# One head's gate projections move from the recurrence to the block stage, by way of DRAM

## The chip, the cores and the metric

The kernel runs on one core of a Trainium2 chip, in float32. The metric is the device time of one execution in microseconds. Five engines work from queues of their own: TensorE (PE; its weight loads are PEld), VectorE (DVE), ScalarE (ACT), GpSimd (POOL) and SyncE (SP), which here only starts transfers. An instruction waits for the semaphores of those it depends on, and the ones behind it on its engine wait with it.

## The reference

One layer of a hybrid encoder block on 1024 tokens of width 1024. One normalised input `h` goes through one wide input projection, whose columns are cut into an attention branch (three groups of eight heads) and a bidirectional gated recurrence of eight heads. The change concerns the recurrence's forget gates, `zf_fwd` and `zf_bwd`:

```
h = rms_norm(h_res, norm_w[layer])
z = einsum('bsd,dc->bsc', h, w_in[layer])
qkv_a, g_a, q_b, zf_fwd, zf_bwd, i_b, g_b, zgate_a, zgate_b = split(z, split_points)
...
def hgrn2_scan(q, i, z_f, lb):
    f = lb + (1.0 - lb) * sigmoid(z_f)
    return gla_chunk_scan(q, 1.0 - f, i, log(f))
o_fwd = hgrn2_scan(q_b, i_b, zf_fwd, lb_f)
o_bwd = flip(hgrn2_scan(flip(q_b), flip(i_b), flip(zf_bwd), lb_b))
o_b = rms_norm(o_fwd + o_bwd, hg_norm_w[layer]) * silu(g_b)
...
merged = sigmoid(zgate_a) * y_a + sigmoid(zgate_b) * y_b
```

`gla_chunk_scan` works on chunks: cumulative sums of the logarithms, products of queries and keys with their exponentials, a state passed from chunk to chunk.

## The kernel before

A float32 product is made from three matmuls of split operands: each operand is a high part (fp32r) and the low rest, and high x high, low x high and high x low are summed. So the 8 blocks of 128 of the inner dimension cost 24 matmuls for each 128 x 512 result.

The stages follow each other on TensorE. First the value projections; then the **block stage** (`run_quads`), in which a "quad", a 2 x 2 block product (two token halves by two column blocks), is made with 7 products of 12 matmuls instead of 8, from sums of the input halves and differences of weight blocks that DVE makes. The block stage makes attention queries and keys, sigmoid gates, SiLU gates and the query projections of six heads of the recurrence, and stores them in DRAM; its list is `blocks`, its weights come in tiles `qraw`, and its results stand in PSUM as `qA`, `qE` and `qC` and leave it as `stage` or `spare`. After it come attention, the merge of its groups, the **recurrence**, and the end stage (projections of both branches, `y_a` first, then the gates and the output product).

In the recurrence TensorE makes, head by head, the four gate projections of a head (two directions `d` by two token halves `u`, `T_group`: 24 matmuls `gp` each). ACT copies each out of PSUM to a tile `sk` of a ring of seven (`evac_f`, `sk_ring`), and after the fourth `start_head` starts the head's chain: ACT makes the sigmoids and, after a change of its function table, the logarithms (`logs`); DVE the running sums (`sums`, tile `Bc`); ACT the exponentials (`exps_b`); DVE the products (`k_mul`, `q_mul`) and, once the decay is known (`decay`), the scaled keys, written over `sk` (`k_state`); TensorE transposes these (`kT`), which frees the `sk` slot, and makes the states (`U`), the products within chunks (`X`, `Y`), the outputs (`oB`) and, after ACT and DVE have normalised them (`on`, `ssb`, `oy`, `oz`), the output transpositions (`onT`). These small products stand between the projections of later heads. Behind the projections of head 7 follow eight groups of the second sigmoid gate (`evac_sg`), and then `y_a`, whose operands (`acc`, split to `xh` and `xl`) are loaded by `end_start`, which runs when all heads are out.

The order on every engine is made while the program is built. A planner (`Plan`) keeps a clock for each engine; tasks and small products (`task`, `product`) are put in when their operands should be there and their ring has room (`soon`); a projection whose result finds no free slot holds the builder at `until`, which lets small products and tasks go ahead. On the chip the order is fixed, and only real dependences make an engine wait.

Heads are counted from 0, so the seventh is head 6. Key transpositions are made strictly in order of the heads (`k_next`). The ring of seven is filled in the order of the `get` calls, so that a tile's slot is that of the tile seven before it. Nearly all instructions are recorded through one helper, line 58, so that the rows of the profile are told apart by the names of their tiles.

Of the kernel before, what the change touches and what calls it, by code (L numbers as in the profile page):

```python
# [8 lines left out]
F32 = mybir.dt.float32  # L9
# [18 lines left out]
TAIL, LATE = 4, 4  # L28
EARLY = 8
QB = 6  # L30
QRAW, SPARE = 6, 7
LOWS = ("T2", "T4")
SQ, EA = 2, 6
# [3 lines left out]
def _dram(ap, offset, dims):  # L37
    return bass.AP(tensor=ap.tensor, offset=ap.offset + offset, ap=dims)
# [584 lines left out]
def hybrid_block(ctx, tc, a, out):  # L623
    b = Builder(ctx, tc, a)
    a_, v_, g_, t_, s_ = b.p.act, b.p.dve, b.p.pool, b.p.pe, b.p.sp
# [4 lines left out]
    dr = ctx.enter_context(tc.tile_pool(name="scratch", bufs=1, space=DRAM))  # L630
# [32 lines left out]
    zf_pages = lambda h: some(head_page(h), 4)  # L663
    ib_pages = lambda k: [_dram(wi, (100 + 40 * k + d) * 65536, [[512, 128], [20 * 65536, 2], [1, 256]]) for d in range(8)]
    q_pages = lambda h: some(head_page(h) + (4 if h % 2 else 12), 2)
    gate_pages = lambda w, j: some((80, 176)[w] + 2 * j, 2)
    qk = [("qk", g, hv, e) for g in range(3) for hv in range(2) for e in range(2)]
    sg = [("sg", 0, j) for j in range(0, 8, 2)] + [("sg", 1, j) for j in range(0, TAIL, 2)]
    blocks = []
    for k in range(6):  # L670
        blocks += qk[2 * k:2 * k + 2] + sg[k:k + 1] + ([("qb", 2 * k - 2)] if 0 < k <= QB // 2 else [])
    blocks += [("gb", k) for k in range(4)] + [("ga", 0), ("ga", 2)]

    def block_pages(kind, *at):
        if kind == "sg":
            return (*gate_pages(*at), *gate_pages(at[0], at[1] + 1))
        if kind == "ga":
            return tuple(some(72 + 2 * at[0], 4))
        if kind == "qb":
            return (*q_pages(at[0]), *q_pages(at[0] + 1))  # L680
        if kind == "gb":
            return tuple(_dram(wi, (100 + 20 * at[0] + 4 * k) * 65536 + 256 + 128 * col, [[512, 128], [65536, 4], [1, 128]])
                         for col in range(2) for k in range(2))
        g, hv, e = at
        p = 24 * g + 8 + 8 * hv
        return tuple(_dram(wi, (p + 4 * k) * 65536 + 128 * (2 * e + col), [[512, 128], [65536, 4], [1, 128]])
                     for col in range(2) for k in range(2))

    items = some(0, 8) + some(24, 8) + some(48, 8)
    items += [block_pages(*x) for x in blocks]  # L690
    for k in range(2):
        items += ib_pages(k)
    for h in range(QB, EARLY):
        items += q_pages(h)
    for j in range(TAIL, LATE):
        items += gate_pages(1, j)
    for h in range(8):
        items += zf_pages(h) + (q_pages(h) if h >= EARLY else [])
    for j in range(LATE, 8):
        items += gate_pages(1, j)  # L700
    items += [wpa[i] for i in range(8)]
# [149 lines left out]
    obD = dr.tile([8, 2, 128, 512], F32, name="obD")  # L851
    ibD = dr.tile([2, 8, 128, 512], F32, name="ibD")
    qD = dr.tile([EARLY, 2, 128, 512], F32, name="qD")
    gbD = dr.tile([8, 2, 128, 512], F32, name="gbD")
    vD = dr.tile([3, S, 512], F32, name="vD")
    qkD = dr.tile([3, 2, 4, 128, S], F32, name="qkD")
# [38 lines left out]
    def T_group(p0, half, evac, last):  # L895
        def step(d):
            wh, wl = b.w[p0 + d // 4]
            c = 128 * (d % 4)
            xh, xl = hs(0, d, 512 * half, 512), hs(1, d, 512 * half, 512)
            return [(wh[:, c:c + 128], xh), (wh[:, c:c + 128], xl), (wl[:, c:c + 128], xh)]  # L900

        gr = dict(k=8, step=step, evac=evac, need=lambda d: p0 + d // 4 + 1)
        if last:
            gr["free"] = lambda d: p0 + (d + 1) // 4
        return gr
# [71 lines left out]
    def root(k):  # L977
        rs[k] = inv_rms(k, bank("ss"))
        rs["d", k] = spread(rs[k])

    def root_out(k):
        rs["B", k] = spread_out(rs["d", k])
# [18 lines left out]
    at = {0: {11: lambda: root(1)}, 3: {5: lambda: root_out(1), 11: lambda: root(0)}, 7: {5: lambda: root_out(0)}}  # L1001
# [174 lines left out]
    def put_raw(dst, silu=False):  # L1176
        def f(half, col, z, mine):
            ring = stage
            if not mine:
                ring, ps, z = blk["spare"], z, blk["spare"].get()  # L1180
                a_.activation(z, ps, AF.Silu if silu else AF.Copy)

            def out():
                s_.dma_start(dst(col, half), z)
                ring.done(z)

            if mine and silu:
                b.task("act", [z], lambda: (a_.activation(z, z, AF.Silu), b.task("sp", [z], out, 1)), 2)
            else:
                b.task("sp", [z], out, 1)  # L1190
        return f

    put_sg = lambda w, j: put_raw(lambda col, half: sgD[w, j + col, half])
    put_ga = lambda j: put_raw(lambda col, half: gaD[j + col, half], True)
    put_qb = lambda h: put_raw(lambda col, half: qD[h + col, half])
    put_gb = lambda k: put_raw(lambda col, half: gbD[2 * k + col, half], True)

    A = {op: [[hq[e][tk][:, c] for c in range(4)] for e in range(2)]
         for op, tk in {"11": (0, 0), "21": (0, 1), "T4": (1, 1)}.items()}
    for op, k in {"T1": 0, "T2": 1, "T3": 2, "22": 3}.items():  # L1200
        A[op] = [[x[:, c] for c in range(4)] for x in blk["S"][k]]
    b.BACK = 1.2
    b.run_quads(A, [{"qk": put_qk, "sg": put_sg, "ga": put_ga, "gb": put_gb, "qb": put_qb}[x[0]](*x[1:]) for x in blocks],
                [blk["spare"] if x[0] == "qk" else stage for x in blocks])
    b.BACK = 2.5
    pos += 7 * len(blocks)
# [377 lines left out]
    for pr in range(2):  # L1584
# [8 lines left out]
        pos += 8  # L1593
    for h in range(QB, EARLY):
        for u in range(2):
# [32 lines left out]
    sk_ring = b.ring(hp, "sk", 7, [128, 512])  # L1628
# [5 lines left out]
    SK, QQ = {}, {}  # L1634

    def evac_f(h, d, u):
        def f(ps):
            t = sk_ring.get()
            a_.activation(t, ps, AF.Copy)
            b.gps.done(ps)  # L1640
            SK[h, d, u] = t
            if d == 1 and u == 1 and h:
                start_head(h)
        return f
# [31 lines left out]
    def load_q_early(h, u):  # L1676
        t = qq_ring.get()
        s_.dma_start(t, qD[h, u])
        QQ[h, u] = t

    def load_gb(h, u):
        t = gb_ring.get()
        s_.dma_start(t, gbD[h, u])
        GB[h, u] = t

    def evac_q(h, u):
        def f(ps):
            t = qq_ring.get()
            a_.activation(t, ps, AF.Copy)
            b.gps.done(ps)  # L1690
            QQ[h, u] = t
        return f

    ORDER = ((0, 0), (0, 1), (1, 1), (1, 0))
# [5 lines left out]
    def start_head(h):  # L1700
        st = dict(used={}, mm=[None, None], G=[None, None], QR={}, Q2={}, KM={}, S={}, s=0, qm=0, km=0)
        H[h] = st
        for d in range(2):
            st["mm"][d] = mm_ring.get()
        b.task("act", [SK[h, d, u] for d, u in ORDER], lambda: logs(h), 4, lambda: qr_ring.soon(4))

    def logs(h):
        for d, u in ORDER:
            a_.activation(SK[h, d, u], SK[h, d, u], AF.Sigmoid)
        ln_exp()  # L1710
        for d, u in ORDER:
            lf = qr_ring.get()
            a_.activation(lf, SK[h, d, u], AF.Ln, scale=omlb[:, d, h:h + 1], bias=lb[:, d, h:h + 1])
            b.task("dve", [lf], lambda d=d, u=u, lf=lf: sums(h, d, u, lf), 4, q2_ring.soon)
# [247 lines left out]
    def load_pair(pr):  # L1962
        for i in range(8):
            b.task("sp", [ibD], lambda i=i: load_ig(pr, i), 4, ig_ring.soon)

    b.low = "dma"
    for h in range(8):
        if h % 2 == 0:
            load_pair(h // 2)
        for u in range(2):  # L1970
            if h < EARLY:
                b.task("sp", [qD], lambda h=h, u=u: load_q_early(h, u), 4, qq_ring.soon)
            b.task("sp", [gbD], lambda h=h, u=u: load_gb(h, u), 4, gb_ring.soon)
        if h == 0:
            start_head(0)
            continue
        for d in range(2):
            for u in range(2):
                b.run_unit([T_group(pos, u, evac_f(h, d, u), u == 1)])
            pos += 2  # L1980
        if h >= EARLY:
            for u in range(2):
                b.run_unit([T_group(pos, u, evac_q(h, u), u == 1)])
            pos += 2
# [423 lines left out]
def _build(arrays):  # L2408
    import concourse.bacc as _bacc
    nc = _bacc.Bacc("TRN2", target_bir_lowering=False, num_devices=1)  # L2410
    args = {n: nc.dram_tensor(f"in_{n}_dram", v.shape, mybir.dt.from_np(v.dtype), kind="ExternalInput").ap()
            for n, v in arrays.items()}
    out = nc.dram_tensor("out_0_dram", (S, D), F32, kind="ExternalOutput").ap()
    with tile.TileContext(nc) as tc:
        hybrid_block(tc, args, out)
    return nc
# [9 lines left out]
```

## Time and profile before

| | |
|---|---|
| median of 2 runs | 1455.42 us (1455.40 to 1455.44) |
| the profiled execution, its own time | 1454.89 us |
| its span, first to last instruction | 1453.1 us |
| instructions | 22946 |
| matmuls | 7930 |
| DMA issues from SP for weight pages of the block stage (`qraw`) | 108 of 256 KB |
| for weight pages of the direct projections (`raw` from `w_in`) | 84 of 256 KB |

In a row of a timeline stand the start in us from the span's start, the length in us, engine, line, operation, output tile <- input tiles, shapes, a count where equal instructions are merged, and in brackets the idle time before it with what ended it. Busy time counts overlapping instructions of one engine once; matmuls overlap, so that the time from the start of one to the start of the next is shorter than the length of one.

### The profile page before, as it was taken

The page shows a single profiled execution, that of the slowest core. Times are in us where ns is not written, and L with a number is a line of the kernel's source. Part 1 is how long each engine was busy: PE and PEld are TensorE (multiplying, and loading weights), DVE is VectorE, ACT ScalarE, POOL GpSimd, SP SyncE. Part 2 cuts the span into 40 slices and gives each one's busy share as a digit, 9 for nine tenths or more (in the row PEclk, how much of TensorE's full clock was granted, in tenths as well). Part 3 has the DMA queues.
Part 4 walks back from the last instruction along what each step waited for, and adds up shares of the span by engine and source line. Part 5 has one row for each costly group of instructions (what it writes and reads, how often), then busy time and mean ns, then how long its engine had stood idle before and what let it go on. Part 6 is the DMA issues. An engine that isn't in the chain of part 4 may idle for free.

```text
span 1453.1 us, 22946 instructions
## 1 busy us (share of the span) xinstructions
PE 1444.3 (99%) x7930; PEld 1197.2 (82%) x7930; DVE 968.1 (67%) x1901; ACT 894.9 (62%) x1900; POOL 340.3 (23%) x356
## 2 busy tenths in 40 slices
PE   9999999999999999999999999999999999999998
PEld 8788888888888888888888778888888888788887
DVE  6673678678685788331564649487878786358973
ACT  7743767466565676443688852497777784558461
POOL 0102434464523433333002000031222221001011
PEclk9999999999999999999999999999999999999999
DMA  7746567777643334324848449354444453778665
GB/s 238 181 143 196 165 195 162 192 153 170 148 123 102 98 105 114 111 102 144 280 144 282 151 118 326 123 141 105 126 109 125 110 138 75 225 240 220 181 154 136
DMA packets 194992, 230.75 MB, mean 159 GB/s; under 512 B 46083, under 2 KB 118043, under 8 KB 194364
## 3 DMA queue, kind: packets, MB, share of 16 engines
q1 hardware_dynamic: 180188, 203.93, 45.0%
q0 software_dynamic: 13824, 25.17, 11.7%
q8 instruction: 62, 1.02, 0.3%
q14 instruction: 54, 0.44, 0.1%
q10 hardware_dynamic: 864, 0.19, 0.1%
HBM read 169.29 MB, written 81.43 MB: 173 GB/s over the span
## 4 chain that ended last, share of the span: by engine, by line
PE 90%; DVE 5%; ACT 3%; DMA 1%; issue 1%; SPq 0%; POOL 0%; ACTq 0%; DVEq 0%
PE gp L58 25%; PE qA L58 20%; PE qE L58 10%; PE sA L58 6%; PE qC L58 5%; PE sE L58 5%; PE u L58 3%; PE o L58 3%; PE oB L58 3%; PE pT L58 2%; PE sc L58 2%; PE nss L58 2%; DVE Bc L58 1%; PE U L58 1%; DVE S L58 1%
## 5 line engine op out<-in xcount | busy, mean ns | idle before, releaser
L58 POOL TENSOR_TENSOR wlo<-qraw,whi 128x512 fp32r<-128x512 f32 x135 | 194.3, 1444 | 381.8 <-ACT whi L58 293.8
L58 ACT ACTIVATE whi<-qraw 128x512 fp32r<-128x512 f32 x189 | 117.7, 626 | 100.8 <-DVE qraw L58 43.1
L58 DVE TENSOR_TENSOR qraw<-qraw,qraw 128x512 f32<-128x512 f32 x108 | 100.0, 927 | 39.0 <-POOL wlo L58 28.0
L58 PE MATMUL gp<-hh,whi 128*128 128x512 f32 x264 | 109.7, 416 | 0.0
L58 PE MATMUL gp<-hh,wlo 128*128 128x512 f32 x264 | 103.6, 393 | 0.0
L58 PE MATMUL gp<-hl,whi 128*128 128x512 f32 x264 | 103.0, 390 | 0.0
L58 ACT ACTIVATE as<-as,neg 128x192 f32<-128x192 f32 (+2 forms) x192 | 83.8, 442 | 16.8 <-DVE neg L58 16.7
L58 ACT ACTIVATE whi<-raw 128x512 fp32r<-128x512 f32 x92 | 57.6, 627 | 43.8 <-PE gp L58 18.7
L58 PE MATMUL qA<-hh,whi 128*128 128x512 f32 x216 | 84.4, 391 | 0.0
L58 PE MATMUL qA<-hh,wlo 128*128 128x512 f32 x216 | 84.3, 390 | 0.0
L58 DVE CUSTOM_DVE_ANT_0 as<-sc,abias 128x192 f32<-128x192 f32 (+2 forms) x192 | 56.0, 348 | 42.4 <-PE sc L58 27.1
L58 PE MATMUL qA<-hl,whi 128*128 128x512 f32 x216 | 84.0, 389 | 0.0
L58 POOL COPY mm<-Bc 128x8 f32<-128x8 f32 x64 | 32.2, 534 | 205.6 <-DVE Bc L58 123.6
L58 PE MATMUL gp<-whi,hh 128*128 128x512 f32 x192 | 78.6, 409 | 0.0
L58 PE MATMUL gp<-wlo,hh 128*128 128x512 f32 x192 | 75.2, 391 | 0.4 <-DVE wlo L58 0.4
L58 PE MATMUL gp<-whi,hl 128*128 128x512 f32 x192 | 75.0, 391 | 0.0
L58 DVE TENSOR_TENSOR wlo<-qraw,whi 128x512 fp32r<-128x512 f32 x54 | 37.3, 691 | 49.6 <-ACT whi L58 49.6
L58 DVE SCALAR_TENSOR_TENSOR ny<-ny,spare 128x512 f32<-128x512 f32 x48 | 67.4, 1405 | 1.6
L58 ACT ACTIVATE ny<-ny 128x512 f32<-128x512 f32 x96 | 60.8, 633 | 4.0 <-DVE ny L58 0.8
L58 PEld LDWEIGHTS gp<-hh,wlo 128*128 128x128 f32 x264 | 49.5, 188 | 11.0
L58 POOL DMA_DIRECT2D wlo<-in_w_in_dram x36 | 31.5, 875 | 113.6 <-ACT wlo L58 97.8
L58 PEld LDWEIGHTS gp<-hh,whi 128*128 128x128 f32 x264 | 49.8, 188 | 8.3
(306 smaller groups left out, 4208.2 us busy)
## 6 DMA issues: line engine op xcount, KB each, us to landing
qraw<-in_w_in_dram SPq DMA_DIRECT2D x108, 256.0 KB, 3.8
raw<-in_w_in_dram SPq DMA_DIRECT2D x84, 256.0 KB, 3.7
qkD<-ny SPq DMA_DIRECT2D x48, 256.0 KB, 2.8
wlo<-in_w_in_dram POOLq DMA_DIRECT2D x36, 256.0 KB, 4.4
sg<-sgD SPq DMA_DIRECT2D x32, 256.0 KB, 3.7
eraw<-wsD SPq DMA_DIRECT2D x32, 256.0 KB, 3.3
sgD<-stage SPq DMA_DIRECT2D x26, 256.0 KB, 2.7
ak<-qkD SPq DMA_DIRECT2D x6, 1024.0 KB, 6.6
```

Source lines behind the costliest of these rows:

```text
L58: got = f(*args, **kw)
```

## The change

The four gate projections of head 6 are made as one quad of the block stage (its two column blocks are the two directions), stored in a DRAM tensor `zfD`, and loaded to `sk` tiles in the recurrence. The loads are tasks of SP with the condition that the ring has room; the head starts when its four tiles are there. The loop of the recurrence goes straight on to head 7. Head 6's four pages of weights leave the list of the direct projections, so the pages behind them move up by four.

```
+ZB = (6,)
...
     for k in range(6):
         blocks += qk[2 * k:2 * k + 2] + sg[k:k + 1] + ([("qb", 2 * k - 2)] if 0 < k <= QB // 2 else [])
+    blocks += [("zf", h) for h in ZB]
     blocks += [("gb", k) for k in range(4)] + [("ga", 0), ("ga", 2)]
...
+        if kind == "zf":
+            return tuple(zf_pages(at[0]))
...
-        items += zf_pages(h) + (q_pages(h) if h >= EARLY else [])
+        items += (zf_pages(h) if h not in ZB else []) + (q_pages(h) if h >= EARLY else [])
...
+    zfD = dr.tile([8, 2, 2, 128, 512], F32, name="zfD")
...
+    put_zf = lambda h: put_raw(lambda col, half: zfD[h, col, half])
...
+    def load_f(h, d, u):
+        t = sk_ring.get()
+        s_.dma_start(t, zfD[h, d, u])
+        SK[h, d, u] = t
+        if all((h, *k) in SK for k in ORDER):
+            start_head(h)
...
         if h == 0:
             start_head(0)
+            continue
+        if h in ZB:
+            for d, u in ORDER:
+                b.task("sp", [zfD], lambda h=h, d=d, u=u: load_f(h, d, u), 4, sk_ring.soon)
             continue
```

The same planner makes a new order of it. On SP, where the kernel before has these rows in the recurrence (stores of outputs `obD`, pages `raw`, gates `gb`, queries `q`, values `ig`):

```order
L58 DMA obD_163<-stage_96_11458 128x512
L58 DMA raw_83_11489<-in_w_in_dram 128x512
L58 DMA gb_11_11491<-gbD_166 128x512
L58 DMA q_12_11538<-qD_165 128x512
L58 DMA q_13_11540<-qD_165 128x512
L58 DMA obD_163<-stage_97_11574 128x512
L58 DMA raw_84_11585<-in_w_proj_a_dram 128x512
L58 DMA gb_12_11587<-gbD_166 128x512
L58 DMA raw_85_11647<-in_w_proj_a_dram 128x512
L58 DMA raw_86_11741<-in_w_proj_a_dram 128x512
```

the changed kernel has these, with the third and fourth of head 6's loads (tiles 28 and 30 of the ring `sk`):

```order
L59 DMA obD_163<-stage_99_11570 128x512
L59 DMA gb_11_11597<-gbD_167 128x512
L59 DMA sk_28_11599<-zfD_166 128x512
L59 DMA q_12_11659<-qD_165 128x512
L59 DMA q_13_11661<-qD_165 128x512
L59 DMA obD_163<-stage_100_11685 128x512
L59 DMA gb_12_11738<-gbD_167 128x512
L59 DMA sk_30_11740<-zfD_166 128x512
L59 DMA raw_83_11803<-in_w_proj_a_dram 128x512
```

Each load stands behind the store of an output and a load of a gate; the page loads have moved, by their four places and behind the loads.

On ACT, the chain of head 6 begins before the change with these rows: the copy of its last projection (tile 27) out of PSUM, a page's split, a table load, and the sigmoids of tiles 24 to 27.

```order
L58 ACTIVATE sk_27_11530<-gp618_11460 128x512
L58 ACTIVATE whi_269_11534<-raw_80_11096 128x512
L58 ACTIVATE wlo_269_11535<-whi_269_11534 128x512
L58 ACT_TABLE_LOAD
L58 ACTIVATE sk_24_11185<-sk_24_11185 128x512
L58 ACTIVATE sk_25_11301<-sk_25_11301 128x512
L58 ACTIVATE sk_27_11530<-sk_27_11530 128x512
L58 ACTIVATE sk_26_11441<-sk_26_11441 128x512
L58 ACT_TABLE_LOAD
```

With the change the sigmoids are those of the loaded tiles 24, 26, 28 and 30, and the copy ahead of them (tile 29) is already that of head 7's third projection.

```order
L59 ACTIVATE sk_29_11735<-gp622_11603 128x512
L59 ACT_TABLE_LOAD
L59 ACTIVATE sk_24_11284<-sk_24_11284 128x512
L59 ACTIVATE sk_26_11381<-sk_26_11381 128x512
L59 ACTIVATE sk_28_11599<-sk_28_11599 128x512
L59 ACTIVATE sk_30_11740<-sk_30_11740 128x512
L59 ACT_TABLE_LOAD
```

Behind them stand the four logarithms (`qr`), of which the next rows show the last, and then, on ACT still, the squares of head 5's two outputs (`on`), the splits of two weight pages (`whi`, `wlo`) and the small steps of the norm (`oy`, `oz`):

```order
L59 ACTIVATE qr_27_11769<-sk_30_11740,lbv_9145,omlb_9146 128x512
L59 ACTIVATE on_10_11789<-oB635_11777 128x512
L59 ACTIVATE whi_275_11797<-raw_79_11194 128x512
L59 ACTIVATE wlo_275_11798<-whi_275_11797 128x512
L59 ACTIVATE on_11_11832<-oB638_11820 128x512
L59 ACTIVATE whi_276_11841<-raw_80_11239 128x512
L59 ACTIVATE wlo_276_11842<-whi_276_11841 128x512
L59 ACTIVATE oy639_11846<-ssb636_11801,eps_82 128x4
```

Then come the small steps of the second output, two sets of four exponentials of head 6 (`km`, `qr`, `q2`), the scalings of head 5's two outputs (`on`) and the exponential of head 6's first decay (`G`). So head 6 now shares its stretch of ACT with head 7's copies, and its sigmoids wait for a transfer, with head 5's outputs behind them.

At the end of the recurrence SP has, before, the last two stores of outputs, a store of the second gate (`sgD`), the loads of the attention's result (`acc`, eight, of which two are shown):

```order
L58 DMA obD_163<-stage_108_12605 128x512
L58 DMA obD_163<-stage_109_12633 128x512
L58 DMA sgD_162<-stage_110_12641 128x512
L58 DMA acc_0_12657<-oaD_161 128x512
L58 DMA acc_1_12659<-oaD_161 128x512
```

and with the change:

```order
L59 DMA sgD_162<-stage_111_12637 128x512
L59 DMA obD_163<-stage_112_12649 128x512
L59 DMA obD_163<-stage_113_12675 128x512
L59 DMA sgD_162<-stage_114_12690 128x512
L59 DMA acc_0_12698<-oaD_161 128x512
L59 DMA acc_1_12700<-oaD_161 128x512
```

Before, one more store of the gate followed behind the eight loads; the last store of the gate stands ahead of them now; on TensorE 30 matmuls of the gate stood behind the last `onT` before the change, and 12 stand there with it.

More of the change, by code (lines that the diff above doesn't have):

```diff
@@ L1202, in hybrid_block @@
     b.BACK = 1.2
-    b.run_quads(A, [{"qk": put_qk, "sg": put_sg, "ga": put_ga, "gb": put_gb, "qb": put_qb}[x[0]](*x[1:]) for x in blocks],
+    b.run_quads(A, [{"qk": put_qk, "sg": put_sg, "ga": put_ga, "gb": put_gb, "qb": put_qb, "zf": put_zf}[x[0]](*x[1:]) for x in blocks],
                 [blk["spare"] if x[0] == "qk" else stage for x in blocks])
```

## The prediction

> **What bounds the kernel now.** I read the page first, then TensorE's matmul rate in the chain of waits, the busy time by stretches of the recurrence, the timelines of TensorE and ScalarE there, and last the hand-over to the end stage.
>
> ```profile
> span 1453.1 us, 22946 instructions
> PE 1444.3 (99%) x7930; PEld 1197.2 (82%) x7930; DVE 968.1 (67%) x1901; ACT 894.9 (62%) x1900; POOL 340.3 (23%) x356
> PE   9999999999999999999999999999999999999998
> ```
>
> TensorE is busy in every slice, so at first sight every matmul saved is time saved. In the chain of waits (start, duration, piece) is the price of one: 24 back to back take 5.44 us in the block stage and 30 take 6.83 us in the recurrence, 0.227 and 0.228 us each (the 390 ns of a group's row is the length of one, and they overlap).
>
> ```profile
> 153.70 5.44 PE qA L58 x24
> 1000.50 6.83 PE gp L58 x30
> ```
>
> The next rows are stretches: length, busy us of PE, PEld, DVE, ACT, POOL with instruction counts, granted clock, DMA. The first is the block stage; the other five run from head 4's first key transposition (kT) to the last output transposition (onT), cut at the kT marks shown below them.
>
> ```profile
> 150.00:680.00 530.00, 530.00 (x2330) 437.05 (x2329) 355.96 (x427) 323.02 (x551) 217.16 (x168) 1.00 0.52 137
> 1103.80:1135.60 31.80, 31.66 (x233) 27.39 (x232) 27.04 (x60) 25.87 (x57) 7.49 (x13) 1.00 0.44 104
> 1135.60:1144.40 8.80, 8.80 (x55) 7.60 (x54) 8.49 (x23) 5.24 (x10) 1.54 (x2) 1.00 0.65 176
> 1144.40:1176.00 31.60, 31.58 (x224) 27.04 (x223) 23.07 (x49) 24.13 (x56) 7.86 (x14) 1.00 0.47 115
> 1176.00:1207.80 31.80, 31.65 (x233) 27.39 (x232) 27.05 (x60) 25.87 (x57) 7.47 (x13) 1.00 0.45 120
> 1207.80:1240.70 32.90, 32.90 (x244) 28.70 (x243) 18.40 (x46) 13.32 (x33) 4.49 (x6) 1.00 0.40 100
> ```
>
> ```profile
> 1135.63 0.60 PE L58 MATMUL kT<-ident,sk 128*128 128x128 f32 x4
> 1144.38 0.49 PE L58 MATMUL kT<-ident,sk 128*128 128x128 f32 x3
> 1176.02 0.93 PE L58 MATMUL kT<-ident,sk 128*128 128x128 f32 x7
> 1207.84 0.60 PE L58 MATMUL kT<-ident,sk 128*128 128x128 f32 x4
> 1240.68 0.60 PE L58 MATMUL onT<-ident,on 128*128 128x128 f32 x4
> ```
>
> In the block stage the other engines have room: DVE 67%, ACT 61%, POOL 41% of 530 us. In the recurrence they have little: DVE is busy for 27.04 of 31.8 us (85%) and ACT for 25.87 (81%), and these two make a serial chain. TensorE's projections are what it does while that chain runs. That is the point of the whole forecast: the two stages are both full of TensorE work, but only in one of them is TensorE alone the limit.
>
> **The block stage: +19.0 us.** One more quad is 84 matmuls: 84 x 0.2267 = 19.04 us, on the path, since TensorE has no gap there. Its other work (7 ACT copies, 5 POOL and 2 DVE subtractions for the low parts, 4 DVE differences, the four results' copies, additions and stores, 4 loads) is hidden under those 19 us, at the shares above; without that cover it would be the POOL's subtractions that show first. The four stores are read only in the recurrence, far behind.
>
> **The recurrence: what goes, and what stays.** Head 6's four groups are 4 x 24 = 96 matmuls, 96 x 0.228 = 21.9 us; ACT loses four copies out of PSUM and eight weight copies, POOL four DMA issues, SP four page loads. If TensorE were all, the kernel would gain 21.9 - 19.0 = 2.9 us. But the ring of projections has 7 slots. By the names in the order, head 6's loads take slots 24, 26, 28 and 30 and head 7's projections 25, 27, 29 and 31, and a slot is free when the key transposition of the tile seven before it is done. So load 30 waits for the last kT of head 5 (tile 23), and head 7's last projection (31) for head 6's first kT (24); the gate pages stand behind that projection in the program, so TensorE can't go on to them. Tile 31 needed tile 24 before as well (head 7's last projection leaves PSUM at 1178.04, after the kT of 1176.02). What is new is that head 6's chain starts with a load that waits for head 5's last kT, while TensorE has 96 matmuls fewer to fill the gap between those two transpositions, 1176.02 - 1144.38 = 31.6 us before.
>
> How long is that gap now? Head 7 shows a head's chain: the last projection out of PSUM, sigmoids, logarithms.
>
> ```profile
> 1178.04 0.60 ACT L58 ACTIVATE sk<-gp 128x512 f32<-128x512 f32 x1
> 1178.66 1.28 ACT L58 ACT_TABLE_LOAD   x1
> 1179.95 2.19 ACT L58 ACTIVATE sk<-sk 128x512 f32<-128x512 f32 x4
> 1182.17 1.28 ACT L58 ACT_TABLE_LOAD   x1
> 1183.46 2.93 ACT L58 ACTIVATE qr<-sk,lbv,omlb 128x512 f32<-128x512 f32 x4
> ```
>
> From the end of that copy (1178.64) to its first kT (1207.84) are 29.2 us, with TensorE full all the time. The other end is ACT's own queue in the changed order. Between the sigmoid of head 6's last load and the exponential of its decay stand a table load, four logarithms, two squares of head 5's outputs, two weight splits (four copies), twice the three small steps of the norm, two sets of four exponentials and two scalings of outputs. The rows for these:
>
> ```profile
> 1165.27 0.49 ACT L58 ACTIVATE km<-qr,lomlb 128x256 f32<-128x256 f32 x1
> 1165.66 0.49 ACT L58 ACTIVATE km<-q,lomlb 128x256 f32<-128x256 f32 x1
> 1166.06 0.61 ACT L58 ACTIVATE qr<-qr 128x512 f32<-128x512 f32 x1
> 1166.58 0.40 ACT L58 ACTIVATE q<-q 128x256 f32<-128x256 f32 x1
> 1167.08 0.60 ACT L58 ACTIVATE on<-oB 128x512 f32<-128x512 f32 x1
> 1167.58 1.14 ACT L58 ACTIVATE on<-oB,oy 128x128 f32<-128x128 f32 x4
> 1168.57 0.32 ACT L58 ACTIVATE oy<-ssb,eps 128x4 f32<-128x4 f32 x1
> 1168.93 0.21 ACT L58 ACTIVATE oy<-oy 128x4 f32<-128x4 f32 x1
> 1169.16 0.21 ACT L58 ACTIVATE oz<-oy 128x4 f32<-128x4 f32 x1
> 1173.46 0.63 ACT L58 ACTIVATE wlo<-whi 128x512 fp32r<-128x512 f32 x1
> ```
>
> The sum: 0.55 + 1.28 + 2.93 + 2 x 0.50 + 4 x 0.63 + 2 x 0.80 + 2 x 1.71 + 2 x 1.14 = 15.6 us, without a gap; at the 81% that is the densest a head's period shows, 19.2 us. The load itself: 0.5 us for the kT that frees its slot, about 1 us for a store and a gate load ahead of it on SP's queue, and 3.9 us to land, as its neighbours on that queue do (issues, KB, median us to landing):
>
> ```profile
> gb<-gbD SPq DMA_DIRECT2D x16, 256.0 KB, 3.9
> ```
>
> So the gap becomes 5.4 + 19.2 = 24.6 us, a gain of 7.0; at the dense end 5.4 + 15.6 = 21.0, a gain of 10.6; at the slow end 5.4 + 29.2 = 34.6, a loss of 3.0. Behind ACT's waiting sigmoid are queued head 5's squares and scalings, for which TensorE's onT waits in order; this is where its idle time will stand. If the store ahead of the load must wait for its own onT, a microsecond or two more goes; I take a gain of 5. Up to head 5's last kT the same number of groups runs as before (head 7's in head 6's place): no gain. After head 6's first kT all work is as before: the 64.7 us to the last onT stay. So of 21.9 us of matmuls, 17 come back as waits.
>
> [...]
>
> **The hand-over to the end: +1.4 us.** After the last onT before, 30 gate matmuls were left, now 12. The loads of the attention's result (acc) are issued when the last recurrence output and the unit running then are through, and on SP behind the store of the gate page.
>
> ```profile
> 1242.28 0.39 PE L58 MATMUL gp<-hh,wlo 128*128 128x512 f32 x1
> 1242.71 0.60 ACT L58 ACTIVATE stage<-gp 128x512 f32<-128x512 f32 x1 [3.57 <-PE gp L58]
> 1243.34 0.32 SPq L58 DMA_DIRECT2D sgD<-stage  x1
> 1243.76 3.71 SPq L58 DMA_DIRECT2D acc<-oaD  x8
> 1246.50 1.31 ACT L58 ACTIVATE xh<-acc 128x512 fp32r<-128x512 f32 x2
> 1250.66 0.50 PE L58 MATMUL gp<-xl,whi 128*128 128x512 f32 x1 [0.22 <-DVE xl L58]
> 1251.93 0.39 PE L58 MATMUL gp<-xh,whi 128*128 128x512 f32 x1
> ```
>
> From the unit's last matmul to the loads: 1243.76 - 1242.28 = 1.48 us; from there to the second group of the attention's projection, which no longer waits, 1251.93 - 1243.76 = 8.17 us. Before, 24 matmuls covered this, and 1251.93 - 1240.68 = 11.25 us passed since the last onT. Now: the transposition 0.36, 12 matmuls to the start of the last 2.6, 1.48 and 8.17: 12.6 us. Without a wait the 24 matmuls of these two steps and the transposition would take 6 us, so TensorE stands still for some 6 us here.
>
> Sum: +19.0 - 5.0 + 1.4 = +15.4 us. On the profiled execution's 1454.89 us (span 1453.1) that is 1470.3; its time is 0.5 under the median of 1455.42, so 1470.8, and I say 1471.
>
> **Rivals.** *The change does what it is for:* chain and ring follow TensorE, as DVE and ACT have idle time on average; then -2.9 + 1.4, 1453.9 us, faster than before. For it: 104.05 us of DVE in the 136.9 us (the five rows' sum) would fit 115. Against it: no head's period is denser than 85% on DVE, and the ring. 8%.
>
> *The late load:* head 6's chain takes its full 29.2 us behind the load, because ACT's and DVE's queues mix it with head 7's and the weight splits: gap 34.6, +19.0 + 3.0 + 1.4 = 23.4, 1478.8 us. It decides when load 30 lands so late that the gap passes 31.6 us. 13%; slower by over 2% (29 us) only if the gap passes 40 us, 5%.
>
> *The clock:* TensorE's waits grow from
>
> ```profile
> PE warm L58 <- DVE warm L58: 1.4, 1, 1.4
> ```
>
> (us, times, longest) to some of 5 or 6 us, and every row of before has the clock at 1.00, so nothing here shows what a long wait does to it. If after each of three such waits some 10 matmuls ran at half rate, 10 x 0.228 = 2.3 us each would be added, most of it where ACT is late anyway but in full at the hand-over: +3 to +6, 1474 to 1477 us. 12%. [...]
>
> **Numbers.** The forecast, 1471, has 67%. Its own bounds are +9.8 (gain 10.6) and +23.4, so 1465 to 1479. The range takes in the clock above and part of the way to the fast rival below: 1461 to 1481. About 2% is what a measurement can tell from no change, 29 us: faster 1%, within 93%, slower 6%.
>
> **What would show it.** Right: TensorE's busy share falls; waits of some us ahead of onT, kT (both by ACT or DVE) around head 6's start, and ahead of the first xh matmul; the gap between head 5's last kT and head 6's first near 25 us; the recurrence ends some 14 us later than before. Wrong: TensorE without idle slices between head 5 and the gates, or a hand-over without a wait, would mean the fast rival; a gap over 32 us the late load; a granted clock under 1.00 the third.

## The result, and the profile after

| | before | after |
|---|---|---|
| median of 2 runs | 1455.42 us | 1475.34 us (1475.11 to 1475.56) |
| span of the profiled execution | 1453.1 us | 1473.3 us |
| instructions; matmuls | 22946; 7930 | 22957; 7918 |

The kernel became slower by 19.9 us, a ratio of 1.0137 (95% interval 1.0120 to 1.0154), with 12 matmuls fewer. The forecast was 1471 us, from 1461 to 1481.

TensorE's row of the busy shares over 40 slices, and its waits (us in total, times, longest), of the changed kernel:

```profile
PE   9999999999999999999999999999999989899999
```

```profile
PE onT L59 <- ACT on L59: 6.9, 2, 6.0
PE gp L59 <- ACT xh L59: 5.3, 1, 5.3
PE oB L59 <- DVE xa L59: 2.0, 1, 2.0
```

The longest wait was 1.4 us before, at the start of the kernel. Now three waits of 2.0 us and more stand in three different slices, and the two longest take their slices from 9 to 8. Two are in the recurrence and one is at the hand-over. Next come the marks in the timeline of TensorE (start, length, and in brackets the wait with what ended it): head 5's first and last kT, the onT that waits, and the first kT of heads 6 and 7.

```profile
1153.70 0.98 PE L59 MATMUL kT<-ident,sk 128*128 128x128 f32 x7
...
1162.45 0.49 PE L59 MATMUL kT<-ident,sk 128*128 128x128 f32 x3
...
1184.74 2.27 PE L59 MATMUL onT<-ident,on 128*128 128x128 f32 x8 [5.97 <-ACT on L59]
1187.37 1.11 PE L59 MATMUL kT<-ident,sk 128*128 128x128 f32 x4 [0.35 <-DVE sk L59]
...
1228.19 0.60 PE L59 MATMUL kT<-ident,sk 128*128 128x128 f32 x4
```

The stretches between these marks, from head 4's first kT to the last onT, answer row by row to the five of before (length, busy us of PE, PEld, DVE, ACT, POOL with counts, granted clock, DMA):

```profile
1123.90:1153.70 29.80, 26.81 (x204) 23.13 (x202) 26.55 (x57) 22.51 (x46) 8.43 (x15) 0.94 0.51 128
1153.70:1162.50 8.80, 8.68 (x50) 7.16 (x51) 8.59 (x24) 4.88 (x15) 0.00 (x0) 1.00 0.28 94
1162.50:1187.40 24.90, 18.48 (x163) 15.88 (x161) 18.09 (x40) 19.68 (x44) 3.98 (x8) 0.91 0.51 137
1187.40:1228.20 40.80, 40.80 (x269) 34.87 (x270) 35.70 (x79) 30.95 (x68) 10.27 (x17) 0.97 0.43 110
1228.20:1257.30 29.10, 29.10 (x226) 25.60 (x225) 14.89 (x37) 10.91 (x28) 2.28 (x3) 1.00 0.30 82
```

Before they were 31.8, 8.8, 31.6, 31.8 and 32.9 us: 136.9 against 133.4 now. TensorE was busy in practically all of the 136.9 us; now it stands still for 9.5 of the 133.4, and three rows have a clock under 1.00. The hand-over, on several engines: the last gate matmul, its copy, its store, the loads of `acc`, the first `xh`, the first and the fifth matmul with an `xh`. (The fifth is the first of `y_a`'s second group.)

```profile
1260.23 0.39 PE L59 MATMUL gp<-hh,wlo 128*128 128x512 f32 x1
...
1260.65 0.60 ACT L59 ACTIVATE stage<-gp 128x512 f32<-128x512 f32 x1 [2.12 <-PE gp L59]
...
1261.76 3.75 SPq L59 DMA_DIRECT2D acc<-oaD  x8
...
1265.25 0.63 ACT L59 ACTIVATE xh<-acc 128x512 fp32r<-128x512 f32 x1 [4.00 <-DMA acc<-oaD]
...
1265.93 0.79 PE L59 MATMUL gp<-xh,whi 128*128 128x512 f32 x1 [5.32 <-ACT xh L59]
...
1271.52 0.47 PE L59 MATMUL gp<-xh,whi 128*128 128x512 f32 x1
```

The first twelve matmuls of `y_a` take 5.59 us, 0.47 each where the block stage has 0.227. The main reason is in the next view, stretches of the same kind around the two long waits; the number before the last two is the granted clock.

```profile
1182.00:1184.00 2.00, 0.00 (x0) 0.00 (x0) 1.36 (x5) 2.00 (x5) 0.00 (x0) 0.74 0.96 242
...
1186.00:1188.00 2.00, 1.65 (x7) 1.18 (x7) 1.92 (x5) 2.00 (x7) 0.58 (x2) 0.50 0.11 34
1188.00:1190.00 2.00, 2.00 (x8) 1.67 (x7) 2.00 (x4) 1.67 (x4) 0.00 (x0) 0.56 0.57 152
...
1264.00:1266.00 2.00, 0.07 (x1) 0.07 (x1) 0.09 (x1) 0.63 (x1) 0.00 (x0) 0.72 0.99 291
...
1268.00:1270.00 2.00, 2.00 (x6) 1.47 (x6) 1.66 (x3) 1.91 (x4) 0.00 (x0) 0.50 1.04 389
1270.00:1272.00 2.00, 2.00 (x7) 1.57 (x6) 2.00 (x4) 1.89 (x4) 0.00 (x0) 0.58 1.06 404
```

In both cases the clock went to half (0.50) while TensorE waited, and it was back 5.1 and 5.8 us after TensorE had work again.

One measure serves all runs below: the **stretch** from head 4's first kT to `y_a`'s second group. It holds all that the change takes away, and none of what it adds. Before and after:

```profile
1103.80:1251.90 148.10, 147.14 (x1029) 126.31 (x1028) 108.12 (x238) 100.68 (x219) 29.72 (x48) 1.00 0.48 124
```

```profile
1123.90:1271.50 147.60, 132.75 (x933) 113.15 (x932) 109.12 (x240) 95.61 (x209) 25.84 (x44) 0.94 0.46 126
```

96 matmuls (21.9 us) are gone from it, and it is 0.5 us shorter. TensorE's busy time fell by 14.4 us, its idle time rose by 13.9.

### The profile page after: what moved, and what is told of

Its sections match the earlier page's. It is cut to its first block, busy times and chain, and to the rows that moved or that the text cites. A ratio compares the mean times of both kernels' runs of the same rounds, so it can differ in the third digit from the quotient of the medians.

```text
span 1473.3 us, 22957 instructions
## 1 busy us (share of the span) xinstructions
PE 1449.2 (98%) x7918; PEld 1199.4 (81%) x7918; DVE 975.6 (66%) x1910; ACT 896.1 (61%) x1899; POOL 342.3 (23%) x357
## 4 chain that ended last, share of the span: by engine, by line
PE 90%; DVE 5%; ACT 3%; issue 1%; DMA 1%; POOL 0%; SPq 0%; ACTq 0%; DVEq 0%; POOLq 0%
PE gp L59 27%; PE qA L59 21%; PE qE L59 10%; PE sA L59 5%; PE qC L59 5%; PE sE L59 4%; PE u L59 3%; PE o L59 3%; PE oB L59 3%; PE pT L59 2%; PE sc L59 2%; PE nss L59 1%; PE U L59 1%; DVE S L59 1%; DVE xs L59 1%
## 5 line engine op out<-in xcount | busy, mean ns | idle before, releaser
L59 POOL TENSOR_TENSOR wlo<-qraw,whi 128x512 fp32r<-128x512 f32 x140 | 198.4, 1421 | 395.5 <-ACT whi L59 312.5
L59 ACT ACTIVATE whi<-qraw 128x512 fp32r<-128x512 f32 x196 | 122.0, 626 | 106.3 <-DVE qraw L59 43.5
L59 DVE TENSOR_TENSOR qraw<-qraw,qraw 128x512 f32<-128x512 f32 x112 | 104.1, 930 | 37.8 <-POOL wlo L59 28.3
L59 PE MATMUL gp<-hh,whi 128*128 128x512 f32 x240 | 100.2, 417 | 0.0
L59 PE MATMUL gp<-hh,wlo 128*128 128x512 f32 x240 | 94.5, 394 | 0.0
L59 PE MATMUL gp<-hl,whi 128*128 128x512 f32 x240 | 94.0, 392 | 0.0
L59 PE MATMUL qA<-hh,wlo 128*128 128x512 f32 x224 | 87.4, 390 | 0.0
L59 ACT ACTIVATE spare<-qA 128x512 f32<-128x512 f32 x52 | 30.9, 593 | 44.8 <-PE qA L59 44.7
L59 PEld LDWEIGHTS gp<-hh,wlo 128*128 128x128 f32 x240 | 45.2, 188 | 10.1
L59 DVE TENSOR_TENSOR_SCAN Bc<-rst,qr 128x512 f32<-128x512 bf16 x32 | 39.0, 1219 | 19.5 <-ACT qr L59 14.3
```

Of the source, the lines that this page charges most:

```text
L59: got = f(*args, **kw)
```

## The experiments

All times are medians. The kernel before ran beside each group on the same chip: 1454.8 us with the first four runs, 1455.64 with the next four, 1455.31 with the two after them, 1455.55 with the last. Single executions of it lay up to 3.8 us from these medians, so small differences are read from the marks of the profiles.

| run | us | ratio to before, 95% interval | stretch, us | clock in it |
|---|---|---|---|---|
| before | | | 148.1 | 1.00 |
| the change | 1475.34 | 1.0137 (1.0120 to 1.0154) | 147.6 | 0.94 |
| 1 block stage alone | 1474.49 | 1.0142 (1.0125 to 1.0159) | 147.5 | 1.00 |
| 2 recurrence alone | 1456.72 | 1.0016 (1.0006 to 1.0026) | 148.9 | 0.94 |
| 3 early hand-over | 1469.99 | 1.0106 (1.0091 to 1.0121) | 142.3 | 0.96 |
| 4 two gate groups in head 6's place | 1471.63 | 1.0115 (1.0100 to 1.0130) | 142.2 | 0.97 |
| 5 useless groups in head 6's place | 1474.18 | 1.0130 (1.0115 to 1.0145) | 146.1 | 1.00 |
| 6 useless group at the hand-over | 1472.72 | 1.0117 (1.0102 to 1.0133) | 146.4 | 0.95 |
| 7 eight slots, two output gates | 1476.22 | 1.0141 (1.0124 to 1.0158) | 148.4 | 0.95 |
| 8 control: two output gates | 1475.99 | 1.0143 (1.0126 to 1.0161) | 149.2 | 0.94 |
| 9 edits of 3 and 4 together | 1460.30 | 1.0031 (1.0021 to 1.0042) | 134.2 | 1.00 |
| 10 head 7 in place of head 6 | 1468.31 | 1.0085 (1.0068 to 1.0102) | 139.1 | 0.96 |
| 11 control: both edits on before | 1460.86 | 1.0047 (1.0029 to 1.0064) | 153.8 | 0.99 |

**1 and 2: each half alone.** In the first, the recurrence's list and loop keep head 6:

```
+ZL = ()
-        items += (zf_pages(h) if h not in ZB else []) + (q_pages(h) if h >= EARLY else [])
+        items += (zf_pages(h) if h not in ZL else []) + (q_pages(h) if h >= EARLY else [])
...
-        if h in ZB:
+        if h in ZL:
```

> Block stage as in the changed kernel (quad for head 6 made and stored), recurrence as in the kernel before (head 6 projected there as well, its stored copy not read). Chain theory (the prediction's): the quad costs its 84 matmuls, 19.05 us by the marks of the two traces, plus the 1.0 us that arose in the attention stage; the recurrence and the hand-over cost what they cost before: 1474.5 to 1475.6 us, no wait of TensorE over 2 us, clock 1.00. Then the whole of the recurrence's side of the change is worth nothing (1475.34 with it). Rival, the moved loads and stores disturb the recurrence and the hand-over and account for the lost 22 us: the quad alone costs 19 us and leaves the marks of the recurrence, but the changed kernel would then differ by waits on DMA. If the quad costs under 15 us (part of it hidden), the forecast's block term is wrong.

In the second, the block stage has no quad, and the loads take stored query projections, so the kernel leaves out head 6's gates:

```
-    blocks += [("zf", h) for h in ZB]
-        s_.dma_start(t, zfD[h, d, u])
+        s_.dma_start(t, qD[h, u])
```

> The other half: no quad in the block stage; head 6's four sk tiles are loaded from the stored query projections of head 6 instead, so that head 6's gate projections are left out of the computation. TensorE does 96 matmuls less than before. Theory that TensorE alone bounds the recurrence: 1455.4 - 21.9 = 1433.5 us. Chain theory, with the sizes of the changed kernel's trace: first kT of head 4 to last onT 133.3 us (-3.5), hand-over 14.3 us (+3.0), rest +0.6: 1455.5 us, within 2 us of before; waits of 6 us ahead of an onT and 5 us ahead of the first xh matmul, clock 0.50 behind them. Late load: over 1459 us.

Measured: 19.7 us over before for the quad alone, and 1.9 us over before with 96 matmuls less. If TensorE's work set the time there, the second would be 21.9 us faster than before. Its largest waits are those of the change:

```profile
PE onT L59 <- ACT on L59: 6.9, 2, 6.0
PE gp L59 <- ACT xh L59: 5.8, 1, 5.8
```

So the quad accounts for the whole loss, and the 21.9 us taken from the recurrence bring nothing. Stores of the new quad that disturb other stages are not needed to explain it.

**5: the same work back, but useless.** Four groups that nobody reads stand where head 6's projections stood:

```
+            for k in range(4):
+                b.run_unit([T_group(pos, k % 2, b.gps.done, False)])
             continue
```

> The changed kernel with four groups of 24 matmuls whose results nobody reads put where head 6's projections stood: 96 matmuls, 21.9 us of TensorE, for nothing. Theory that the removed projections were only filler: the waits ahead of onT, oB and xh vanish, the clock is back at 1.00, and the time stays within 2 us of the changed kernel's on the same chip (19 to 22 us over the kernel before). TensorE bound: 20 us or more over the changed kernel. Something between, by the part that was not filler: the 3.5 us that the recurrence gained come back, and the 3.0 us of the hand-over go.

Measured: 18.5 us over before, so no slower than the change although TensorE does 21.9 us more. The stretch shows TensorE busy again all the time, at full clock, and 1.5 us shorter than in the change:

```profile
1125.80:1271.90 146.10, 145.96 (x1029) 126.61 (x1028) 109.20 (x241) 95.98 (x210) 26.55 (x44) 1.00 0.45 121
```

So as the program stood, the removed projections were filler: with useless work in their place the stretch is no longer than with nothing there. (The order differs in one more way: head 6's last load is issued 6.2 us ahead of head 5's last kT here, at 1160.18 and 1166.37, and behind it in the change. Runs 7 and 8 look at the load.) The part about "what was not filler" missed: no 3.5 us came back.

**7 and 8: is it the ring?** The eighth slot is paid for with one of the output gates' three, hence the control:

```
-    sk_ring = b.ring(hp, "sk", 7, [128, 512])
+    sk_ring = b.ring(hp, "sk", 8, [128, 512])
-    gb_ring = b.ring(hp, "gb", 3, [128, 512])
+    gb_ring = b.ring(hp, "gb", 2, [128, 512])
```

> The changed kernel with eight slots for sk tiles in place of seven, paid for with two slots instead of three for the output gates (its control is the next run). Theory that the ring keeps head 6's loads back (the prediction's reading: load 30 waits for head 5's last kT): with eight slots load 30 waits for the kT before that one, ACT's sigmoid comes some 4 us earlier, the gap of 24.9 us between head 5's last kT and head 6's first becomes 20 to 22 us, and 3 to 5 us go against the control. Rival, the chain of DVE and ACT sets the pace and the ring follows it: the gap stays within 1.5 us, and so does the time.

> Control for the run with eight slots: the changed kernel with two slots instead of three for the output gates, nothing else. Both theories: within 1.5 us of the changed kernel; if it is slower by more, the output gates' loads come late at the onT and the eight-slot run is to be read against this one.

Measured: 1476.22 against 1475.99, the same. The issues of SP and the timeline of TensorE with eight slots show the last load of head 6, the last kT of head 5 and the first of head 6:

```profile
1156.93 0.38 SPq L59 DMA_DIRECT2D sk<-zfD  x1
...
1174.41 0.83 PE L59 MATMUL kT<-ident,sk 128*128 128x128 f32 x3 [1.98 <-DVE sk L59]
...
1194.75 0.60 PE L59 MATMUL kT<-ident,sk 128*128 128x128 f32 x4
```

In the changed kernel that load is issued behind head 5's last kT. Here are DVE's last step for the output that is stored ahead of it, SP's three issues, and the sigmoid on ACT that waits for the load:

```profile
1165.24 0.74 DVE L59 SCALAR_TENSOR_TENSOR stage<-onT,onw,gb 128x512 f32<-128x512 f32 x1
...
1166.01 0.32 SPq L59 DMA_DIRECT2D obD<-stage  x1
1166.38 0.61 SPq L59 DMA_DIRECT2D gb<-gbD  x1
1167.08 0.41 SPq L59 DMA_DIRECT2D sk<-zfD  x1
...
1170.01 0.63 ACT L59 ACTIVATE sk<-sk 128x512 f32<-128x512 f32 x1 [3.01 <-DMA sk<-zfD]
```

So it was not the ring that held this load on the chip. The kT that frees its slot ended at 1162.94, and SP stood until 1166.01 before the store, 3.5 us of it waiting for DVE's `stage` by the list of SP's waits; the load came right behind. The ring acts earlier: it decides where the planner puts the load in SP's order.

With eight slots the load goes 17.5 us ahead of head 5's last kT instead of 4.6 behind it, and the gap is 20.3 us in place of 24.9, as the ring's theory said. But that kT now comes 49.6 us after head 4's first (1124.80), in the change 38.5 (1162.45 - 1123.92), so head 6's first kT comes later all the same. An earlier load without other filler was worth nothing in this run. The planner also put the work of heads 5 and 6 in another order for eight slots, so why head 5 became late is not shown.

**3 and 4: where the filler stands.** First the last gate unit is held back until all heads are out:

```
+            if (j, half) == (7, 0):
+                b.until(lambda: all(st.get("f", 0) == 2 for st in H.values()))
             if not ectx and all(st.get("f", 0) == 2 for st in H.values()):
                 end_start()
```

> The changed kernel with the last gate unit held back until all heads are out, so that the loads of the attention's result are issued before it and not after it: 24 gate matmuls behind the last onT instead of 12, and the loads beside them. Chain theory: the wait of 5.3 us ahead of the first xh matmul falls to under 1.5 us, a wait of 1 to 2 us appears ahead of the last onT, the clock stays above 0.90 between the last onT and the end stage, and 3 to 5.5 us go: 1470 to 1472.5 us. If the hand-over's extra 3.0 us came from DMA alone (loads slow to land) and not from cover and clock, under 1.5 us go.

Then, in the other run, two gate groups go into head 6's place (and their pages with them in `items`):

```
+            for j in range(LATE, LATE + FILL):
+                for half in range(2):
+                    b.run_unit([T_group(pos, half, evac_sg(1, j, half), half == 1)])
+                pos += 2
             continue
...
-    for j in range(LATE, 8):
+    for j in range(LATE + FILL, 8):
```

> The changed kernel with two of the eight gate groups (48 matmuls, the fifth page pair of the second gate) made in head 6's place instead of behind head 7. No matmul more or less; only where the filler stands. Theory that the removed projections were filler for the DVE and ACT chain: waits ahead of kT, onT and oB in heads 5 and 6 shrink by some 3 to 6 us, part of it given back at the end, where only six gate groups are left for the hand-over: 1469 to 1474 us. Rival, the ring of seven slots and the load that waits for the last kT of head 5 set the gap of 24.9 us between that kT and head 6's first: the gap and the waits stay, and with less cover at the end the time is 1475 to 1478 us.

Measured against 1454.8: 15.2 us and 16.8 us slower, where the change is 19.9 slower: 4.7 and 3.1 us won, both about as expected. With the early hand-over the last onT and the start of the second group are

```profile
1255.56 0.59 PE L59 MATMUL onT<-ident,on 128*128 128x128 f32 x2 [0.51 <-ACT on L59]
...
1266.56 0.40 PE L59 MATMUL gp<-xh,whi 128*128 128x512 f32 x1
```

11.0 us instead of 14.3. With the moved groups the wait ahead of onT in head 6 is gone, and so is part of the gap, 22.1 us with more of TensorE's work in it:

```profile
1163.92 0.49 PE L60 MATMUL kT<-ident,sk 128*128 128x128 f32 x3
...
1185.99 0.60 PE L60 MATMUL kT<-ident,sk 128*128 128x128 f32 x4
```

This does not clear the load, though, because the planner put it earlier too: the last one is issued 6.0 us ahead of head 5's last kT.

```profile
1157.95 0.39 SPq L60 DMA_DIRECT2D sk<-zfD  x1
```

Run 4 changes the place of the filler and of the load together, and how much of the 2.8 us belongs to which is not shown. At the end, where the groups were taken from, TensorE now waits 3.0 us ahead of the last onT and 5.4 us ahead of the first `xh`.

**6: keeping the clock up.** One useless group stands behind the last gate group:

```
-            b.run_unit([T_group(pos, half, evac_sg(1, j, half), half == 1)])
+            b.run_unit([T_group(pos, half, evac_sg(1, j, half), half == 1 and j < 7)])
...
+            if (j, half) == (7, 1):
+                b.run_unit([T_group(pos, half, b.gps.done, True)])
```

> The changed kernel with one group of 24 matmuls whose result nobody reads behind the last gate group, in the 5.3 us in which TensorE waits for the first xh. Theory that the halved clock costs time at the hand-over: the clock stays 1.00 there, the first y_a group runs at 0.23 us a matmul as far as its operands are there, and the second begins 1.0 to 1.4 us earlier (ACT's third xh stands at 1267.68 us in the changed kernel, so not more): 1 us under the changed kernel, with 24 matmuls more. Rival, ACT and DMA set the pace of that group and the clock does not matter: no gain, or a loss of up to 0.5 us, since the useless group ends a little after the first xh is there.

Measured: 17.1 us over before. In the profile the clock is at full rate at the hand-over, and the second group starts at 1268.16, 11.8 us after the last onT (1256.33) instead of 14.3. The rows are ACT's first two `xh`, the first matmul of the second group, and a stretch of 4 us between the marks:

```profile
1263.68 1.23 ACT L59 ACTIVATE xh<-acc 128x512 fp32r<-128x512 f32 x2 [0.17 <-DMA acc<-oaD]
...
1268.16 0.39 PE L59 MATMUL gp<-xh,whi 128*128 128x512 f32 x1
...
1264.00:1268.00 4.00, 3.87 (x17) 2.75 (x17) 3.15 (x5) 3.18 (x6) 0.68 (x1) 1.00 0.94 324
```

From ACT's first `xh` to the second group the changed kernel took 1271.52 - 1265.25 = 6.3 us, this one 1268.16 - 1263.68 = 4.5. Of these 1.8 us 0.6 can be the loads', since the third `xh` stands 2.4 us behind the first in the change (1267.68) and 1.8 here (1265.48); so 1.2 to 1.8 us of the 2.4 belong to the clock, and the rest to loads that came earlier. The stretch is only 1.2 us shorter, since the recurrence ended 1.3 us later here: by the lengths of the matmuls' rows, TensorE worked at half rate for some 7.0 us behind the wait at head 6 (1182.91 to about 1189.9), in the change for 5.1. The medians point the same way, but their intervals overlap, so a gain in time is not shown.

**9 and 11: both edits, on the change and on the kernel before.** The diffs are those of 3 and 4.

> Both earlier edits together: two gate groups in head 6's place and the last gate unit held back until all heads are out. The stretch from head 4's first kT to the second y_a group was 147.6 us in the changed kernel, 142.3 with either edit alone. If the two gains were independent they add to some 10 us; they share the gate groups, so theory says 6 to 9 us under the changed kernel: 1466.5 to 1469.5 us, with no wait over 3 us and the clock above 0.95. Not below the kernel before (1455): the block stage's 19 us stay, and of the 21.9 us removed the 5 to 6 that the waits and the slow clock take at most can come back beside the 0.5 of the stretch. If it beats 1457 us, the theory that the removed matmuls were mostly filler is wrong.

> Control on the kernel before: the same two edits as in the run with both (two gate groups moved ahead of head 6's projections, the last gate unit held back until all heads are out), with head 6 still projected in the recurrence. If the edits are gains of their own, the kernel before gains too (some 5 us or more: 1450 us or less), and the run with both says little about the moved projections. Theory: before has no wait over 1.4 us there, so the edits have nothing to fill; the gate groups are only taken from the end: between 0 and 6 us slower, 1455 to 1461 us.

Measured: 5.0 us over before on the change, and 5.3 us over before on the kernel before. The first expectation is missed by more than 6 us: the gains do not overlap, they more than add up. The stretch shows why, first of the kernel before with both edits, then of the change with them:

```profile
1103.80:1257.60 153.80, 149.44 (x1029) 127.69 (x1028) 108.52 (x239) 100.55 (x220) 29.68 (x48) 0.99 0.48 121
...
1123.00:1257.20 134.20, 128.46 (x934) 108.95 (x933) 108.05 (x238) 93.45 (x206) 26.19 (x44) 1.00 0.49 128
```

The same matmuls as in the change (933 or 934 recorded) are done in 128.46 us of busy time at clock 1.00, where the change needed 132.75 at 0.94. The difference of 4.3 us is put down to the slow clock. (As an estimate from the other side: TensorE is busy for 13.3 us of the change's half-rate stretches, so at most 6.6 us can be lost there.) Idle time falls from 14.9 to 5.7 us, the longest wait behind the start-up is 1.1 us, and the clock stays at 1.00. The control says the rest. The edits are no gain of their own: on the kernel before they cost 5 us. And between these two kernels, which have the moved gate groups in the same places, moving head 6 shortens the stretch from 153.8 to 134.2 us, by 19.6 of the 21.9, which repays the quad. Part of that repairs what the edits cost the kernel before: against its own stretch of 148.1 us it is 13.9 us, less than the quad costs. No run beat the kernel before. (The load of head 6 comes early in run 9 as in run 4; run 7, where it does so without the filler, is the only sign that this is not what wins.)

**10: another head.** `ZB = (7,)`, nothing else.

> The last head (head 7) moved to the block stage in place of head 6; all else as in the changed kernel. Then no head's projection stands behind the stored one, and the gate groups come right behind head 6's projections. Theory of lost filler: the 96 matmuls are missing wherever they are taken from, so the time is within 6 us of the changed kernel (1469 to 1477 us), with the waits now in the last head's chain and at the hand-over. Rival, what costs is the place of head 6 (its loads in turn with head 7's projections in one ring): with the loads last in the ring the recurrence gains its 21.9 us but for the hand-over, 1457 to 1460 us.

Measured: 13.0 us over before, 7 less than with head 6; the value is a little under the range of the filler theory and far over that of the rival. The waits stand where no projection is left, at the end (2.5 us ahead of the last onT and 5.4 ahead of `xh`). So what is lost depends on which head's filler is missing.

## Why the prediction was right, point by point

**The block stage, +19.0: right.** The first matmul of the stage to the last `qA` step took 537.3 us before (142.7 to 680.0) and 556.4 after (142.5 to 698.9): 19.1. The quad alone is 19.7 us by the medians. About 1 us more stands in the change's profile between the block stage and attention's first outputs. That piece varies from execution to execution (below) and is no cost of the change.

**The recurrence, a gain of 5.0: the cause right in the main, the size 3.5, and all three steps off.** The gap between head 5's last and head 6's first kT was forecast at 24.6 us and is 24.9, but that nearness is luck, since two errors cancel. From that kT to the sigmoid of the last load 7.6 us passed (1170.01 - 1162.45), forecast 5.4: what came on top is the store's wait for its own onT, which the prediction put into its gain (5 instead of 7) and not into the gap. From the sigmoid to head 6's first kT it took 17.4 us, forecast 19.2: up to the end of the decay's exponential (1186.59) ACT was busy for 14.9 of 16.6 us, 90%, and not the 81% that it was given. The other two steps failed openly. "Up to head 5's last kT no gain" failed, since that part became 2.0 us shorter (40.5 to 38.5), and "the 64.7 us to the last onT stay" failed, since it took 69.9. The row from 1187.40 shows TensorE busy there all the time with 269 matmuls where 233 stood: what it could not do while it waited, it did later, part of it at half clock. And the gap itself does not decide: run 7 shortens it by 4.6 us and gains nothing.

**The hand-over, +1.4: mis-sized, +3.0.** From the last onT (1257.26) to the second group it took 14.26 us, forecast 12.6. The steps up to the first `xh` matmul came as worked out (wait of 5.3 us, forecast about 6); the rest is mainly `y_a`'s first group at half clock, for which run 6 gives 1.2 to 1.8 us.

**The clock: right as a rival, and left out of the sum.** It was given 3 to 6 us and 1474 to 1477 us; it is 4.3 us of TensorE's busy time by the comparison with run 9, and the time fell into that range. The forecast's 1471 lacks this term. From the marks: +20.1 up to head 4's first kT, -3.5, +3.0, and +0.6 in the end stage, 20.2 us in all. Against the forecast's +15.4 that is 1.5 us less gain, 1.6 more at the hand-over, and 1.7 that lie in the scatter and the end stage. Nothing ties the last to the clock, so that the time lies in this rival's range is partly chance.

The trace of the change has a half-rate stretch at each of the three waits. TensorE had 5.1 and 5.8 us of work behind the long waits before the clock was back, and a wait of 2.0 us too was followed by such a stretch (last section). No run shows the rival's ten matmuls at half rate behind each wait: the change's three half-rate stretches hold 14, 16 and 13 matmuls as recorded, with TensorE busy for 2.8, 4.7 and 5.8 us.

**The rivals.** That the change does what it is for (1453.9) is refuted for this program by run 2, which lacks the quad and gains nothing; but run 9 shows that it was no law of the chain. DVE, busy for 85% of the densest head's period before the change and for 73% of the whole stretch (108.12 of 148.1 us), is at 81% over the stretch of run 9 (108.05 of 134.2 us) against 74% in the change (109.12 of 147.6). The prediction's reading, that ACT's and DVE's chain has no room, went too far: there was room, but TensorE's remaining work was not where the chain left it free. The late load (1478.8) did not happen.

## What to carry to other kernels

Where TensorE's work covers another engine's chain, a matmul that is taken out may save nothing until other TensorE work is moved into the hole. Here the saving was 0.5 of 21.9 us without moving any, and 13.9 with it. To ask whether work is filler before planning its removal, put useless work of the same length in its place, or take it out alone: here both runs gave the answer. And the waits on TensorE cost more than their own length here: behind those of 2.0, 6.0 and 5.3 us the clock was at half for 3.4, 5.1 and 5.8 us, to which 4.3 us of TensorE's busy time are put down by the comparison with run 9.

## What the runs showed of the hardware

**Three waits, three stretches at half clock.** From the granted clock in narrow windows of the change's trace, the stretches at half rate (0.50) can be placed: 1148.8 to 1152.2, 1183.0 to 1189.8 and 1264.9 to 1271.7 us. (A clock of 0.70 over 2 us is 1.2 us at half rate, so the first begins at 1148.8.) They last 3.4, 6.8 and 6.8 us. In the same way two stretches of run 7 last 3.4 us each (from 1154.0 and from 1174.5) and one of run 4 lasts 10.2 (from 1255.8). The first of the change follows a wait of only 2.00 us, and begins 1.2 us after TensorE has work again (1147.61):

```profile
1146.00:1148.00 2.00, 0.40 (x3) 0.40 (x4) 1.92 (x5) 1.97 (x5) 0.40 (x1) 1.00 0.33 36
1148.00:1150.00 2.00, 2.00 (x15) 2.00 (x15) 1.93 (x8) 0.92 (x4) 0.00 (x0) 0.70 0.53 96
1150.00:1152.00 2.00, 1.60 (x8) 1.30 (x7) 1.97 (x4) 0.36 (x1) 0.71 (x2) 0.50 0.00 0
1152.00:1154.00 2.00, 1.41 (x7) 0.88 (x8) 2.00 (x5) 2.00 (x8) 1.26 (x4) 0.94 0.00 0
```

In run 9, with no wait over 1.1 us behind the start-up, the clock stayed at 1.00. What sets the start and the length of such a stretch is not shown.

**The start of attention scatters.** From the block stage's last `qA` group (its first high product) to the first output of attention, executions of these kernels took between 32.6 and 36.2 us (33.7 in the kernel before, 34.8 in the change), with the same work in it. In the longest TensorE waited 2.3 us for a load of queries. A difference of 1 to 2 us between two profiles can come from there; what else sets it is not shown.
